# A hybrid encoder layer: the output projection's attention side takes its first two column blocks as a pair, one quarter of it in seven products

## The chip, the cores and the metric

The kernel runs on one core of a Trainium2 chip. A core has a matrix engine (TensorE, PE in the profile, its weight loads are PEld), a vector engine (VectorE, DVE), an activation engine (ScalarE, ACT), a general engine (GpSimd, POOL) and a queue engine that issues DMAs (SyncE, SP). Data lies in SBUF, 128 partitions wide; matmuls write to PSUM, in banks of 128 x 512 float32. The metric is device time in microseconds (us), the median of several runs of one launch.

## The reference

One layer over 256 rows of width 2048. It is a half feed-forward (FFN1), a mixer with two sides that read one projection, an output projection, a second half feed-forward (FFN2) and a gated embedding. The part that matters here is the output projection:

```python
        mixed = jnp.concatenate([rms_norm(y_ssm, out_norm_ssm[i]), rms_norm(y_sb, out_norm_sb[i])], axis=-1)
        x = x + mixed @ w_out[i]
```

`y_ssm` and `y_sb` are 256 x 1024 each (the SSM side and the attention side), `w_out` is 2048 x 2048, all of it in float32. Each side is normalized by its own row-wise root mean square.

## The kernel before

**Products.** A float32 operand is kept as two parts: a high part, and the remainder of the value against it. A product of two operands is three matmuls: high by high, low by high, high by low. Activations lie turned in such pairs (`nhi`, `nlo`, or `hhi`, `hlo`). Weights come in raw quarters, 512 rows by 512 columns as a tile of 128 x 2048 (1 MB), by a DMA on SP (line 331); each quarter has two halves of 128 x 1024. For each half `split` makes the high part by a cast on ACT (line 182) and the remainder by a subtraction on DVE (line 185). The raw tiles are a ring of five, two of which are in use for the rows of x, so that three go round.

**The ring of pairs.** `weight_pair` hands out the tiles for (high, remainder) of a half: four pairs with names `whi`, `wlo` from the pool `wp`, and, where `ring` holds another pool, three more pairs `shi`, `slo` from that one, in turn. The FFNs use all seven; the output projection uses four. `ring` is a list of that other pool and a counter.

**Blocks.** `gemm_block` computes a column block of 512 columns for both row blocks (256 rows) into two PSUM banks of the four single ones (`acc`): for a side of 1024 rows of weights that is two quarters, four halves, and 12 matmuls to a half, 48 in all. `gemm_half` orders them: high weights with both parts of the activations (line 346), then remainder weights with the high part (line 341). `gemm_pair` computes two column blocks at once, in all four single banks.

**Seven products.** The class `Seven` computes two column blocks of one quarter of the rows as a 2 x 2 by 2 x 2 block product in seven products (of 6 matmuls each) instead of eight. It needs sums of the weight tiles (`add`, line 541; one by an accumulating DMA on POOL) and sums of the activations: `whole_rows` (line 470) adds the parts of a quarter, `sum_forms` (line 487) makes four sums of its 128 x 256 pieces and splits them. `Seven.lean` is the variant in single banks: ACT copies (line 606) and DVE adds carry intermediate results out of a bank that is used three times. Its `column` computes a quarter in the ordinary way into the same banks. Line 533 and its neighbours are its matmuls. Before, the mixer's projection for v uses `lean`, in `values()` (its adds stand around line 1638), and FFN1, FFN2 and the last stage use `chunk`, with double banks.

**Order.** The code is recorded, and a scheduler sets the order on each engine. `put_off(n, ...)` puts a piece of work off by n steps of the weight stream; `pin` keeps an instruction where it was written. Each engine then runs its list in order and waits by semaphores.

**Around the change.** `glu` ends the SSM side and gives `yss`, `attn_out` the attention side, `ysb` (each a list of two quarters). `rms(steps, ...)` computes a side's row scale: ones-matmuls, a copy out of PSUM (line 1500) and a chain of small DVE operations (lines 205 to 213). The squares it needs are made on ACT (line 1511) and added on POOL (line 1512). Then `gemm_pair` runs over the SSM side's column blocks 0 and 1, and six `gemm_block` follow: (block 0, attention), (1, attention), (2, SSM), (2, attention), (3, SSM), (3, attention). Behind each of the eight block results x += result * scale runs on DVE (line 1673), which frees the bank. When a column block of x is complete, POOL stores it, and its normalized form for FFN2 is prepared (`n2.block`: transposes on DVE at line 220, splits at lines 195 and 197). FFN2 starts behind the last block.

Of the kernel before, what the change touches and what calls it, by code (L numbers as in the profile page):

```python
# [13 lines left out]
ALU = mybir.AluOpType  # L14
AX = mybir.AxisListType

P = 128
# [9 lines left out]
NB = 512  # L27
# [6 lines left out]
def layer_kernel(ctx: ExitStack, tc: tile.TileContext, a: dict, shapes: dict, out: bass.AP):  # L34
    nc = tc.nc
    _, T, D = shapes["x"]
    F = shapes["ffn1_w_gate"][2]
    SW = shapes["ssm_d"][1]
# [5 lines left out]
    TT = T // P  # L44
# [9 lines left out]
    wp = ctx.enter_context(tc.tile_pool(name="wts", bufs=4))  # L54
# [15 lines left out]
    def com(tag):  # L70
        return get(comp, tag, *{"sg": (1024, 1), "h": (1024, 2), "sq": (NB, 1), "mid": (2048, 1)}[tag])
# [36 lines left out]
    def put_off(steps, fn, *args):  # L108


        def g():
            for _ in range(steps):
                yield
            fn(*args)

        return start(g())
# [183 lines left out]
        return both[:2], both[2:]  # L300

    ring = [None, 0]

    def weight_pair():

        extra, i = ring
        ring[1] += 1
        pool, tags = (extra, ("shi", "slo")) if extra and i % 7 % 2 else (wp, ("whi", "wlo"))
        return [
            pool.tile([P, 2, NB], F32R, tag=s, name=uid(s), bufs=3 if pool is extra else None) for s in tags  # L310
        ]
# [44 lines left out]
    def gemm_block(act, w, n0, nkt, first=()):  # L356

        ps = [acc(), acc()]
        for k0 in range(0, nkt, 4):
            part = act(k0 // 4)  # L360
            quarter = first[k0 // 4] if k0 // 4 < len(first) else weight_halves(w, k0, min(4, nkt - k0), n0)
            for half in list(quarter):
                k = k0 + 2 * half[0]
                gemm_half(ps, (part, half), range(TT), k == 0, k + 2 == nkt, in_turn=first and k0 == 0)
                if first and half[0] == 0 and k0 + 4 < nkt:
                    act(k0 // 4 + 1)
                step()
        return ps

    def gemm_pair(act, ws, nkt):  # L370


        ps = [[acc(), acc()] for _ in ws]
        last = nkt // 4 - 1
        for ks in (range(last - 1), (last - 1,), (last,)):
            for (w, n0), banks in zip(ws, ps):
                for k in ks:
                    part = act(k)
                    for half in list(weight_halves(w, 4 * k, 4, n0)):
# [21 lines left out]
    class Normed:  # L401


        def __init__(self, gain, laid=None, kinds="nnnn", late=1):
            self.early = ND - late
            self.kinds = kinds
            self.gain = gain
            self.laid = laid
            self.parts = {}
            self.mid = None  # L410
            self.ss = [small(ND) for _ in range(TT)]
            self.r = None
# [65 lines left out]
    def sum_forms(pool, u, kind="n"):  # L478

        sums = pool.tile([P, 2, NB], F32, tag="sum", name=uid("rows"), bufs=2)  # L480
        s = sums.rearrange("p j n -> p (j n)").rearrange("p (z j x b) -> p z j x b", z=4, j=2, b=32)
        (a11, a21), (a12, a22) = ([u[:, k : k + 2, 4 * t : 4 * t + 4] for t in range(TT)] for k in (0, 2))
        for z, (x, y, op) in enumerate((
            (a21, a22, ALU.subtract), (s[:, 0], a11, ALU.subtract),
            (a11, a21, ALU.subtract), (a12, s[:, 1], ALU.add),
        )):
            nc.vector.tensor_tensor(out=s[:, z], in0=x, in1=y, op=op)
        both = halves(kind)
        split(*both, sums.rearrange("p j n -> p (j n)").rearrange("p (z t) -> p z t", z=4))
        return both  # L490
# [662 lines left out]
    class Spare:  # L1153
# [5 lines left out]
        def tile(self, shape, dtype, tag, name, bufs):  # L1159
            return get(self.pool, "rt", bufs=3).rearrange("p (j n) -> p j n", n=NB)  # L1160
# [221 lines left out]
    qT, kT, vt = [None, None], [None, None], [None, None]  # L1382
# [223 lines left out]
    q0, k0, v0 = SW, SW + NH * DH, SW + 2 * NH * DH  # L1606
    mix, s5p, atp = ExitStack(), ExitStack(), ExitStack()
    mixp = mix.enter_context(phase("mix"))
    pool = s5p.enter_context(phase("s5"))

    s5_main(pool, mixp)
    forms = {}
# [7 lines left out]
    pool = atp.enter_context(phase("attn"))  # L1620
    zs, ysb = [], []
# [4 lines left out]
    put_off(16, attn_out, pool, 0, ysb, sqa)  # L1626
    vt = [get(pool, f"v{t}") for t in range(TT)]

    def values():
        even, odd = ([v[:, n * NB : (n + 1) * NB] for v in vt] for n in range(2))  # L1630

        def scaled(n):
            for t in range(TT):
                v = vt[t][:, n * NB : (n + 1) * NB]
                pin(nc.scalar.activation(v, v, AF.Copy, scale=nm.rs(t)))

        def halfway(s):
            nc.vector.tensor_tensor(out=even[0], in0=s.bank(2), in1=even[0], op=ALU.add)

        def done(s):  # L1640
            nc.vector.tensor_tensor(out=even[1], in0=s.bank(4), in1=odd[1], op=ALU.add)
            for t in range(TT):
                nc.vector.tensor_tensor(out=odd[t], in0=s.bank(5), in1=odd[t], op=ALU.subtract)
            put_off(1, scaled, 0)

        def ended(s):
            for t, z in enumerate((3, 8)):
                nc.vector.tensor_tensor(out=odd[t], in0=s.bank(z), in1=odd[t], op=ALU.add)
            put_off(1, scaled, 1)

        class Rows:

            def tile(self, shape, dtype, tag, name, bufs):
                return com("h").rearrange("p (j n) -> p j n", n=NB)

        s = Seven(nm, forms.get, ((w_in, v0), (w_in, v0 + NB)), Rows(), None)
        s.column(0, (0, 1, 3))
        s.lean(2, even[0], *odd, halfway, done)
        s.column(1, (0, 1, 3), True)
        put_off(0, ended, s)  # L1660
# [3 lines left out]
    yss, rss = glu(pool, zs)  # L1664
    rsb = rms(9, sqa, NH * DH)
    KS = SW // NB
    sides = [a["w_out"][:, side * KS : (side + 1) * KS] for side in range(2)]
    both = gemm_pair(lambda k: yss[k], [(sides[0], n * NB) for n in range(2)], SW // P)
    for n, side in ((0, 0), (1, 0), (0, 1), (1, 1), (2, 0), (2, 1), (3, 0), (3, 1)):
        y, r = ((yss, rss), (ysb, rsb))[side]  # L1670
        ps = next(both) if n < 2 and not side else gemm_block(lambda k: y[k], sides[side], n * NB, SW // P)
        for t in range(TT):
            nc.vector.scalar_tensor_tensor(
                out=xt[t][n], in0=ps[t], scalar=r[0][:, t : t + 1], in1=xt[t][n], op0=ALU.mult, op1=ALU.add
            )
        if side:
            for t in range(TT):
                nc.gpsimd.dma_start(scr_x[t * P : (t + 1) * P, n * NB : (n + 1) * NB], xt[t][n])
            put_off(0 if n == ND - 1 else 2, n2.block, n)
    atp.close()  # L1680
    mix.close()

# [96 lines left out]
    t = 0  # L1779
# [159 lines left out]
```

## Time and profile before

| | |
|---|---|
| median of 3 runs | 1812.14 us (1811.14 to 1813.1) |
| the profiled execution | 1811.75 us, span 1810.0 us |
| SSM pair's last matmuls end | 956.54 us |
| attention block 0 begins, block 1, (2, SSM), (2, attention), (3, SSM) | 956.61, 968.18, 979.07, 989.95, 1000.83 us |
| FFN2's first matmul | 1022.59 us |
| DVE busy, 956 to 1022 | 50.28 us of 66.00 |
| a weight quarter of `w_out`, from issue to landing | 4.6 to 6.6 us, median 5.0 |

A row of the timeline reads: start, duration, engine, line, operation, output <- inputs with shape and type, how many were put together, and in brackets the idle time before and what ended it. A row of a group reads: line, engine, operation, names, shapes and count, then busy time and mean duration, then the idle time just before these instructions and what ended it. Starts of long neighbouring DVE operations are some 0.08 us closer than their durations, since the end of one overlaps the start of the next.

### The profile page before, as it was taken

How to read it: one execution, taken by the hardware profiler on the slowest of the kernel's cores; microseconds unless marked ns; L12 is line 12 of the kernel's file. 1: busy time of each engine (PE TensorE's matmuls, PEld its weight loads, DVE VectorE, ACT ScalarE, POOL GpSimd, SP SyncE). 2: the span in 40 equal slices, each digit the busy share in tenths (PEclk: the TensorE clock that was granted, in tenths of full speed). 3: DMA queues.
4: the chain of work that ended last, by engine and by line, in shares of the span. 5: the costliest groups of instructions: out<-in, count | busy, mean ns of one | idle time of the engine just before them, and what ended most of it. 6: DMA issues, size and time to landing. Idle time of an engine off the chain costs nothing.

```text
span 1810.0 us, 24253 instructions
## 1 busy us (share of the span) xinstructions
PE 1803.4 (100%) x8902; PEld 1494.9 (83%) x8902; DVE 1598.2 (88%) x1870; ACT 1077.4 (60%) x1253; POOL 132.7 (7%) x194
## 2 busy tenths in 40 slices
PE   9999999999999999999999999999999999999998
PEld 7888888888888888888898888888888888888887
DVE  7998889999998898887867899999999999889775
ACT  7445456556565666466895566555565566567664
POOL 0020100000000001112221000000000000000000
PEclk9999999999999999999999999999999999999999
DMA  9599867787776666765646777786767786666563
GB/s 377 209 310 303 253 226 233 238 270 223 258 267 221 193 238 222 257 240 179 203 155 211 242 284 235 259 263 230 233 232 245 238 272 244 223 207 226 198 244 128
DMA packets 108087, 429.46 MB, mean 237 GB/s; under 512 B 24544, under 2 KB 48384, under 8 KB 65568
## 3 DMA queue, kind: packets, MB, share of 16 engines
q1 hardware_dynamic: 95808, 390.10, 61.1%
q0 software_dynamic: 11872, 37.50, 9.6%
q8 instruction: 70, 1.15, 0.3%
q14 instruction: 49, 0.40, 0.1%
q10 hardware_dynamic: 288, 0.31, 0.1%
HBM read 372.41 MB, written 10.88 MB: 212 GB/s over the span
## 4 chain that ended last, share of the span: by engine, by line
PE 98%; DMA 1%; DVE 0%; SPq 0%; ACT 0%; issue 0%; DVEq 0%; ACTq 0%
PE acc L346 31%; PE acc L341 16%; PE aux L346 15%; PE aux L341 8%; PE acc L530 5%; PE acc L535 5%; PE acc L533 5%; PE aux L533 3%; PE aux L535 3%; PE aux L530 3%; DMA raw<-in_ffn_w_gate 1%; PE aux L1318 0%; PE acc L1575 0%; PE acc L1570 0%; PE acc L1566 0%; PE aux L1263 0%
## 5 line engine op out<-in xcount | busy, mean ns | idle before, releaser
L185 DVE TENSOR_TENSOR wlo<-raw,whi 128x1024 fp32r<-128x1024 f32 x478 | 577.1, 1221 | 103.9 <-ACT whi L182 101.2
L182 ACT CAST whi<-raw 128x1024 fp32r<-128x1024 f32 x478 | 496.4, 1050 | 285.2 <-PE acc L346 166.1
L346 PE MATMUL acc<-whi,nhi 128*128 128x512 f32 x852 | 334.1, 393 | 0.6 <-ACT whi L182 0.5
L346 PE MATMUL acc<-whi,nlo 128*128 128x512 f32 x852 | 331.5, 390 | 0.0
L341 PE MATMUL acc<-wlo,nhi 128*128 128x512 f32 x852 | 240.9, 389 | 0.0
L185 DVE TENSOR_TENSOR slo<-raw,shi 128x1024 fp32r<-128x1024 f32 x186 | 226.4, 1217 | 16.0 <-ACT shi L182 15.7
L182 ACT CAST shi<-raw 128x1024 fp32r<-128x1024 f32 x186 | 195.3, 1050 | 62.2 <-DMA raw<-in_ffn_w_down 23.2
L346 PEld LDWEIGHTS acc<-whi,nhi 128*128 128x128 f32 x852 | 159.9, 188 | 35.7 <-ACT whi L182 0.9
L341 PEld LDWEIGHTS acc<-wlo,nhi 128*128 128x128 f32 x852 | 159.9, 188 | 33.6 <-DVE wlo L185 0.2
L346 PEld LDWEIGHTS acc<-whi,nlo 128*128 128x128 f32 x852 | 160.3, 188 | 32.6
L182 ACT CAST whi<-sum 128x1024 fp32r<-128x1024 f32 x79 | 83.2, 1053 | 156.8 <-DVE sum L541 138.8
L182 ACT CAST shi<-sum 128x1024 fp32r<-128x1024 f32 x59 | 62.2, 1053 | 101.5 <-DVE sum L541 86.8
L634 POOL DMA_DIRECT2D raw<-raw x45 | 39.3, 873 | 1041.6 <-DVE sum L541 691.1
L541 DVE TENSOR_TENSOR sum<-sum,raw 128x1024 f32<-128x1024 f32 x92 | 112.3, 1220 | 0.9
L185 DVE TENSOR_TENSOR wlo<-sum,whi 128x1024 fp32r<-128x1024 f32 x79 | 96.3, 1221 | 5.2 <-ACT whi L182 4.5
L346 PE MATMUL aux<-whi,nhi 128*128 128x512 f32 x244 | 95.0, 390 | 0.0
L346 PE MATMUL aux<-whi,nlo 128*128 128x512 f32 x244 | 95.0, 389 | 0.0
L341 PE MATMUL aux<-wlo,nhi 128*128 128x512 f32 x244 | 75.1, 389 | 0.0
L185 DVE TENSOR_TENSOR slo<-sum,shi 128x1024 fp32r<-128x1024 f32 x59 | 72.1, 1221 | 1.0 <-ACT shi L182 0.5
L346 PE MATMUL acc<-whi,hhi 128*128 128x512 f32 x156 | 60.7, 389 | 0.0
L346 PE MATMUL acc<-whi,hlo 128*128 128x512 f32 x156 | 60.7, 389 | 0.0
L541 DVE TENSOR_TENSOR sum<-raw,raw 128x1024 f32<-128x1024 f32 x46 | 56.1, 1219 | 4.0 <-DMA raw<-in_ffn_w_down 3.1
(423 smaller groups left out, 3531.2 us busy)
## 6 DMA issues: line engine op xcount, KB each, us to landing
raw<-in_ffn_w_up SPq DMA_DIRECT2D x88, 1024.0 KB, 5.5
raw<-in_ffn_w_down SPq DMA_DIRECT2D x88, 1024.0 KB, 4.8
raw<-in_ffn_w_gate SPq DMA_DIRECT2D x86, 1024.0 KB, 7.1
raw<-in_w_in SPq DMA_DIRECT2D x32, 1024.0 KB, 5.6
raw<-raw POOLq DMA_DIRECT2D x48, 512.0 KB, 5.9
raw<-in_w_out SPq DMA_DIRECT2D x16, 1024.0 KB, 5.0
raw<-in_w_ple_gate SPq DMA_DIRECT2D x16, 1024.0 KB, 5.0
hT<-mid SPq DMA_DIRECT2D x160, 64.0 KB, 4.5
```

Of the source, the lines that this page charges most:

```text
L182: copy = nc.scalar.copy(hi, src)
L185: rest = nc.vector.tensor_tensor(out=lo, in0=src, in1=hi.bitcast(F32), op=ALU.subtract)
L341: nc.tensor.matmul(ps[t], lhsT=lh, rhs=lo[:, j, cols], start=False, stop=stop and j == 1)
L346: nc.tensor.matmul(ps[t], lhsT=(ahi, alo)[i][:, 2 * h + j, t * P : (t + 1) * P], rhs=hi[:, j, cols], start=start and j == 0 and i == 0, st ...
L530: nc.tensor.matmul(ps, lhsT=lh[j], rhs=hi[:, j], start=begin and j == 0, stop=False, skip_group_check=joined)
L533: nc.tensor.matmul(ps, lhsT=ll[j], rhs=hi[:, j], start=False, stop=False, skip_group_check=joined)
L535: nc.tensor.matmul(ps, lhsT=lh[j], rhs=lo[:, j], start=False, stop=z in final and j == 1, skip_group_check=joined)
L541: nc.vector.tensor_tensor(out=t, in0=x, in1=y, op=ALU.add)
L634: nc.gpsimd.dma_start(b12, b22, accum_op=ALU.add)
```

## The change

Two things change in the output projection, and the rest moves behind them.

The ring gets six pairs instead of four: `Lent` hands out two more pairs from the tiles of q and k (`q0`, `k0`, `q1`, `k1`), which are no longer used by then, and `extra_of` replaces the fixed seven. Behind the output projection it is set back.

The attention side's blocks 0 and 1 become one pair, `first_two`: the second quarter of the rows by `column` for both blocks (2 x 24 matmuls), the first quarter by `lean` (7 products of 6 matmuls), between the two columns. The forms of `ysb[0]` are made ahead of it, and both `gathered` of the SSM pair are called ahead of it too, with what was the loop's body before. The results are added up in the tiles of v, which are free by then, and x += result * scale follows as before.

```diff
     ring = [None, 0]
+    extra_of = [7, 7]
...
-        pool, tags = (extra, ("shi", "slo")) if extra and i % 7 % 2 else (wp, ("whi", "wlo"))
+        pool, tags = (extra, ("shi", "slo")) if extra and i % extra_of[0] % 2 and i % extra_of[0] < extra_of[1] else (wp, ("whi", "wlo"))
...
-    both = gemm_pair(lambda k: yss[k], [(sides[0], n * NB) for n in range(2)], SW // P)
-    for n, side in ((0, 0), (1, 0), (0, 1), (1, 1), (2, 0), (2, 1), (3, 0), (3, 1)):
-        y, r = ((yss, rss), (ysb, rsb))[side]
-        ps = next(both) if n < 2 and not side else gemm_block(lambda k: y[k], sides[side], n * NB, SW // P)
+    class Lent:
+        def __init__(self):
+            self.tags = ["q0", "k0", "q1", "k1"]
+            self.i = 0
+
+        def tile(self, shape, dtype, tag, name, bufs):
+            self.i += 1
+            return mixp.tile(shape, dtype, tag=self.tags[self.i % 4 - 1], name=name, bufs=1)
+
+    def gathered(n, side, ps):
+        r = (rss, rsb)[side]
         for t in range(TT):
             nc.vector.scalar_tensor_tensor(
                 out=xt[t][n], in0=ps[t], scalar=r[0][:, t : t + 1], in1=xt[t][n], op0=ALU.mult, op1=ALU.add
...
+    def first_two():
+        even, odd = ([v[:, n * NB : (n + 1) * NB] for v in vt] for n in range(2))
+
+        def halfway(s):
+            nc.vector.tensor_tensor(out=even[0], in0=s.bank(2), in1=even[0], op=ALU.add)
+
+        def done(s):
+            nc.vector.tensor_tensor(out=even[1], in0=s.bank(4), in1=odd[1], op=ALU.add)
+            for t in range(TT):
+                nc.vector.tensor_tensor(out=odd[t], in0=s.bank(5), in1=odd[t], op=ALU.subtract)
+            put_off(1, gathered, 0, 1, even)
+
+        def ended(s):
+            for t, z in enumerate((3, 8)):
+                nc.vector.tensor_tensor(out=odd[t], in0=s.bank(z), in1=odd[t], op=ALU.add)
+            gathered(1, 1, odd)
+
+        forms = {}
+        s = Seven(lambda k: ysb[k], forms.get, ((sides[1], 0), (sides[1], NB)), Rows(), None)
+        forms[0] = sum_forms(s.pool, whole_rows(s.pool, ysb[0]), "h")
+        for n in range(2):
+            gathered(n, 0, next(both))
+        s.column(0, (1,))
+        s.lean(0, even[0], *odd, halfway, done)
+        s.column(1, (1,), True)
+        put_off(0, ended, s)
+
+    ring[:], extra_of[:] = [Lent(), 0], [6, 4]
+    both = gemm_pair(lambda k: yss[k], [(sides[0], n * NB) for n in range(2)], SW // P)
+    first_two()
+    for n, side in ((2, 0), (2, 1), (3, 0), (3, 1)):
+        y = (yss, ysb)[side]
+        gathered(n, side, gemm_block(lambda k: y[k], sides[side], n * NB, SW // P))
+    ring[0], extra_of[:] = None, [7, 7]
```

`Rows`, which gives `Seven` a common buffer `h` for its sums, moves out of `values()` so that both can use it.

What becomes of the order is seen on three places. First DVE, from the copy of a mean square out of PSUM to the first x += result * scale of the SSM pair. Before (`wlo` is a weight remainder, `sm` the small operands of the scale, `acc` the bank, `x` the rows):

```order
L1500 COPY sm_8504<-aux_8501 128x2
L185 TENSOR_TENSOR wlo_8585<-raw_8578,whi_8584 128x1024
L205 TENSOR_SCALAR sm_8506<-sm_8504 128x2
L208 RECIPROCAL sm_8508<-sm_8508 128x2
L210 TENSOR_TENSOR sm_8511<-sm_8508 128x2
L211 TENSOR_TENSOR sm_8511<-sm_8511,sm_8506 128x2
L212 TENSOR_SCALAR sm_8511<-sm_8511 128x2
L213 TENSOR_TENSOR sm_8508<-sm_8508,sm_8511 128x2
L1673 SCALAR_TENSOR_TENSOR x_4227<-acc_8372,sm_8508,x_4227 128x512
```

The same place on DVE after the change (`h_8642`, `h_8667`, `h_8691` are the weight sums t1, t2, t4; `slo_8680` is a remainder in a lent tile, the one that `slo_8536` of the SSM pair's last half used before it):

```order
L205 TENSOR_SCALAR sm_8517<-sm_8515 128x2
L185 TENSOR_TENSOR wlo_8657<-h_8642,whi_8656 128x1024
L542 TENSOR_TENSOR h_8667<-h_8642,raw_8640 128x1024
L208 RECIPROCAL sm_8519<-sm_8519 128x2
L542 TENSOR_TENSOR h_8691<-h_8667,raw_8638 128x1024
L210 TENSOR_TENSOR sm_8522<-sm_8519 128x2
L185 TENSOR_TENSOR wlo_8670<-raw_8638,whi_8669 128x1024
L211 TENSOR_TENSOR sm_8522<-sm_8522,sm_8517 128x2
L185 TENSOR_TENSOR slo_8680<-h_8667,shi_8679 128x1024
L212 TENSOR_SCALAR sm_8522<-sm_8522 128x2
L213 TENSOR_TENSOR sm_8519<-sm_8519,sm_8522 128x2
L1684 SCALAR_TENSOR_TENSOR x_4227<-acc_8383,sm_8519,x_4227 128x512
```

One operation of 128 x 1024 stood there, and now five do, two of them the sums t2 and t4.

Second PE, at the seam from the SSM pair to the attention side. Before:

```order
L341 MATMUL acc_8375<-wlo_8525,nhi_8344 128x512
L346 MATMUL acc_8576<-whi_8580,nhi_8122 128x512
L346 MATMUL acc_8576<-whi_8580,nlo_8123 128x512
L346 MATMUL acc_8577<-whi_8580,nhi_8122 128x512
L346 MATMUL acc_8577<-whi_8580,nlo_8123 128x512
```

And after:

```order
L342 MATMUL acc_8386<-slo_8536,nhi_8344 128x512
L347 MATMUL acc_8597<-whi_8589,nhi_8551 128x512
L347 MATMUL acc_8597<-whi_8589,nlo_8552 128x512
L342 MATMUL acc_8597<-wlo_8590,nhi_8551 128x512 x2
L347 MATMUL acc_8604<-whi_8589,nhi_8551 128x512
```

The attention side now begins with its second quarter (`nhi_8551`, where `nhi_8122` was the first), a row block at a time.

Third DVE at the start of FFN2, from the last x += result * scale on (`mid` are turned rows, `nlo` of `rows` the remainder of a sum form, `wlo` of `raw` remainders of FFN2's first weights). Before:

```order
L1673 SCALAR_TENSOR_TENSOR x_4227<-acc_9014,sm_8619,x_4227 128x512
L1673 SCALAR_TENSOR_TENSOR x_4228<-acc_9015,sm_8619,x_4228 128x512
L220 STREAM_TRANSPOSE mid_8992<-x_4227 128x4x4x32
L220 STREAM_TRANSPOSE mid_8992<-x_4228 128x4x4x32
L185 TENSOR_TENSOR wlo_9185<-raw_9178,whi_9184 128x1024
L455 TENSOR_REDUCE sm_9209<-sm_111 128x1
```

And after:

```order
L1684 SCALAR_TENSOR_TENSOR x_4227<-acc_9035,sm_8630,x_4227 128x512
L1684 SCALAR_TENSOR_TENSOR x_4228<-acc_9036,sm_8630,x_4228 128x512
L220 STREAM_TRANSPOSE mid_9009<-x_4227 128x4x4x32
L185 TENSOR_TENSOR nlo_9163<-rows_9157,nhi_9162 128x1024
L220 STREAM_TRANSPOSE mid_9009<-x_4228 128x4x4x32
L185 TENSOR_TENSOR wlo_9216<-raw_9213,whi_9215 128x1024
L185 TENSOR_TENSOR wlo_9220<-raw_9213,whi_9219 128x1024
L456 TENSOR_REDUCE sm_9244<-sm_111 128x1
```

A form's remainder, which stood ahead of the last block's results, now stands between the two transposes, and two weight remainders stand where one did.

More of the change, by code (lines that the diff above doesn't have):

```diff
@@ L1627, in layer_kernel @@
     vt = [get(pool, f"v{t}") for t in range(TT)]
+    class Rows:
+        def tile(self, shape, dtype, tag, name, bufs):
+            return com("h").rearrange("p (j n) -> p j n", n=NB)
     def values():
@@ L1649, in ended @@
             put_off(1, scaled, 1)
-        class Rows:
-            def tile(self, shape, dtype, tag, name, bufs):
-                return com("h").rearrange("p (j n) -> p j n", n=NB)
         s = Seven(nm, forms.get, ((w_in, v0), (w_in, v0 + NB)), Rows(), None)
@@ L1667, in layer_kernel, with tile @@
     sides = [a["w_out"][:, side * KS : (side + 1) * KS] for side in range(2)]
-    both = gemm_pair(lambda k: yss[k], [(sides[0], n * NB) for n in range(2)], SW // P)
-    for n, side in ((0, 0), (1, 0), (0, 1), (1, 1), (2, 0), (2, 1), (3, 0), (3, 1)):
-        y, r = ((yss, rss), (ysb, rsb))[side]
-        ps = next(both) if n < 2 and not side else gemm_block(lambda k: y[k], sides[side], n * NB, SW // P)
+    class Lent:
+        def __init__(self):
+            self.tags = ["q0", "k0", "q1", "k1"]
+            self.i = 0
+        def tile(self, shape, dtype, tag, name, bufs):
+            self.i += 1
+            return mixp.tile(shape, dtype, tag=self.tags[self.i % 4 - 1], name=name, bufs=1)
+    def gathered(n, side, ps):
+        r = (rss, rsb)[side]
         for t in range(TT):
```

## The prediction, made before the changed kernel ran

> **What bounds the kernel now.** I read the page's totals first, then its clock slices and the chain that ended last.
>
> ```profile
> span 1810.0 us, 24253 instructions
> ...
> PE 1803.4 (100%) x8902; PEld 1494.9 (83%) x8902; DVE 1598.2 (88%) x1870; ACT 1077.4 (60%) x1253; POOL 132.7 (7%) x194
> ...
> PEclk9999999999999999999999999999999999999999
> ...
> PE 98%; DMA 1%; DVE 0%; SPq 0%; ACT 0%; issue 0%; DVEq 0%; ACTq 0%
> ```
>
> PE never stops: its busy time is the span, at an undiminished granted clock, and the chain is PE for 98%. So a matmul taken away counts in full, and any new wait of PE counts in full too. DVE is second with 88%. The view of PE's waits says how little PE waits for others:
>
> ```profile
> PE aux L252 <- POOL ones L125: 1.1, 1, 1.1
> PE acc L346 <- ACT whi L182: 0.5, 1, 0.5
> ```
>
> Next the stretch of the change, by windows (columns: length, then busy time of PE, PE's weight loads, DVE, ACT, POOL, the clock, DMA).
>
> ```profile
> 956.00:1022.00 66.00, 65.92 (x293) 54.19 (x292) 50.28 (x66) 33.44 (x47) 3.32 (x6) 1.00 0.68 227
> ```
>
> PE is full; DVE has 66.00 − 50.28 = 15.7 us left over. PE's timeline gives the pace and the two seams:
>
> ```profile
> 955.47 1.07 PE L341 MATMUL acc<-wlo,nhi 128*128 128x512 f32 x4
> 956.61 0.47 PE L346 MATMUL acc<-whi,nhi 128*128 128x512 f32 x1
> ...
> 968.18 0.39 PE L346 MATMUL acc<-whi,nhi 128*128 128x512 f32 x1
> ...
> 979.07 0.39 PE L346 MATMUL acc<-whi,nhi 128*128 128x512 f32 x1
> ```
>
> The SSM pair ends at 955.47 + 1.07 = 956.54, and the attention side's column block 0 follows at 956.61. A block of 48 matmuls lasts 979.07 − 968.18 = 10.89 us, so one costs 0.2269 us.
>
> **What it removes.** Column blocks 0 and 1 of the attention side had 2 × 48 = 96 matmuls. Now: two columns of 24 and seven products of 6, 90 in all. Six fewer: 6 × 0.2269 = **−1.36 us**. Block 0 before took 968.18 − 956.61 = 11.57 us, of which four small matmuls of the next mean square are some 0.36; the other 0.3 us are little hiccups at its beginning. They go if operands are waiting when PE comes late: **−0.3 us**.
>
> **What it adds.** Durations come from the same operations elsewhere: the pair for v (862 to 877), and FFN2's forms.
>
> ```profile
> L185 DVE TENSOR_TENSOR wlo<-raw,whi 128x1024 fp32r<-128x1024 f32 x25 | 30.3, 1218 | 11.3 <-ACT whi L182 11.3
> L470 DVE TENSOR_TENSOR whole<-hhi,hlo 128x1024 f32<-128x1024 f32 x1 | 1.2, 1225 | 0.0
> L487 DVE TENSOR_TENSOR rows<-whole 128x256 f32<-128x256 f32 x2 | 0.8, 416 | 0.0
> ...
> 862.05 1.23 DVE L541 TENSOR_TENSOR h<-raw,raw 128x1024 f32<-128x1024 f32 x1 [0.49 <-DMA raw<-in_w_in]
> ...
> 876.39 0.68 DVE L1638 TENSOR_TENSOR v<-acc,v 128x512 f32<-128x512 f32 x1
> ...
> L606 ACT COPY v<-acc 128x512 f32<-128x512 f32 x1 | 0.6, 587 | 0.0
> ...
> L599 POOL DMA_DIRECT2D raw<-raw x1 | 0.9, 940 | 3.5 <-ACT sp L1449 3.5
> ```
>
> DVE: a whole (1.22), four form subtractions (4 × 0.42), the form's remainder (1.22), t1, t2, t4 (3.7), three more weight remainders (eleven instead of eight, 3.7) and six adds (6 × 0.68): about 15.6 us. ACT: one form cast and three weight casts of 1.05, three copies of 0.59: 6.0 us. POOL: one issue of 0.94, landing while PE waits or works on other products; I count nothing for it, and 0.9 us if a product stood waiting for it. About 5.3 us of DVE's share (whole, forms, t1) falls before 956, the other 10.3 into a stretch with 15.7 to spare. As a sum DVE holds. What costs is **where** it stands.
>
> **The new wait.** PE's first attention matmul writes a bank that the first `gathered` of the SSM pair must read. DVE before, up to that operation:
>
> ```profile
> 940.85 6.79 DVE L185 TENSOR_TENSOR wlo<-raw,whi 128x1024 fp32r<-128x1024 f32 x5 [1.69 <-ACT whi L182]
> 949.54 1.66 DVE L197 SCALAR_TENSOR_TENSOR nlo<-aux,gains,nhi 128x256 fp32r<-128x256 f32 x4 [1.90 <-ACT nhi L195]
> 951.12 0.16 DVE L1500 COPY sm<-aux 128x2 f32<-128x2 f32 x1
> 951.19 1.22 DVE L185 TENSOR_TENSOR wlo<-raw,whi 128x1024 fp32r<-128x1024 f32 x1
> ...
> 954.05 0.17 DVE L208 RECIPROCAL sm<-sm 128x2 f32<-128x2 f32 x1 [1.02 <-ACT sm L207]
> ...
> 955.71 2.73 DVE L1673 SCALAR_TENSOR_TENSOR x<-acc,sm,x 128x512 f32<-128x512 f32 x4
> ```
>
> Before, one large operation stands between the mean square's copy and `gathered`; after, five (the order shown with the change), each 1.14 us from start to start (951.19 to 952.33 in the DVE timeline). They are not free to go early. t1 needs the attention pair's second quarter, whose raw buffer is refilled only when `slo_8536`, a remainder of the SSM side, has been taken. The last of the five, `slo_8680`, goes into the lent slot that PE reads until the end of the SSM pair. The rows for the walk:
>
> ```profile
> 938.54 1.33 ACT L1511 ACTIVATE sqp<-h 128x256 f32<-128x256 f32 x4
> ...
> 939.09 4.06 POOL L1512 TENSOR_TENSOR sqg<-sqg,sqp 128x256 f32<-128x256 f32 x4 [12.99 <-ACT sqp L1511]
> 951.76 3.70 POOL L1512 TENSOR_TENSOR sqa<-sqa,sqp 128x256 f32<-128x256 f32 x4 [8.60 <-ACT sqp L1511]
> ...
> DMA to landing us min/median/max: 4.6/5.0/6.6
> ```
>
> 1. One more weight cast stands ahead of the squares on ACT, so they end at 938.54 + 1.33 + 0.95 = 940.8; the form's buffer is theirs until then.
> 2. DVE then does four form subtractions (1.5) and three remainders at the 6.79 / 5 = 1.36 that this row shows beside POOL's adds (4.1): `slo_8536` is done at about 946.4.
> 3. The quarter lands 5.0 later, 951.4; t1 takes until 952.5; four nlo (1.66), the copy and a small one: 954.3.
> 4. Five large operations, 5 × 1.14 = 5.7, small ones between them 0.4, and 1.0 for POOL's second group of adds, now beside them: 961.4.
> 5. `gathered` needs 0.70 (2.73 / 4): PE resumes at 962.1 and not at 956.61: **+5.5 us**.
>
> Lower end: were everything early, `slo_8680` still follows PE's end at 956.54: 1.22, two small ones and 0.70 give 959.1, so 2.5 us. Upper end: 1.6 more for a DMA at its longest (6.6) and 1.0 for another cast in the way: 8.1. I take the walk's 5.5, each step of which has a row. What lies behind the waiting DVE operation is all of PE's work; nothing else covers it.
>
> A rule bears on step 4. The Trainium skill, "SBUF — State Buffer", section "SBUF: two separate sides", says that DVE operations with two SBUF inputs and GpSimd exclude each other for whole instructions. The row agrees in kind (1.36 instead of 1.14 beside the adds); taken in full, all 3.70 us of adds would block DVE, and the sum would be 2.7 us higher than with my 1.0.
>
> **Behind it.** The middle of the pair: product 3 gets a bank that the `halfway` add frees, queued on DVE behind the late remainders: **+0.4 us** (0 if PE's delay has let DVE catch up). FFN2's start: two transposes are split by a form remainder that before had been done, and remainders of its first weights stand behind it.
>
> ```profile
> 1022.56 1.41 DVE L1673 SCALAR_TENSOR_TENSOR x<-acc,sm,x 128x512 f32<-128x512 f32 x2 [0.56 <-PE acc L341]
> ...
> 1037.55 1.22 DVE L185 TENSOR_TENSOR slo<-sum,shi 128x1024 fp32r<-128x1024 f32 x1
> ...
> 1038.82 0.73 PE L535 MATMUL acc<-slo,hhi 128*128 128x512 f32 x2
> ```
>
> DVE does 1.2 to 2.4 us more between the last `gathered` and that remainder. Already before, the remainder that ends at 1037.55 + 1.22 = 1038.77 is what the matmul at 1038.82 takes. Some idle slivers of DVE and late starts of PE cover part: **+0.6 us**, from 0 to 2.
>
> **Sum**, against the profiled execution's 1811.75 (its span and 1.75 around it; 0.39 under the median 1812.14): 1811.75 − 1.36 − 0.3 + 5.5 + 0.4 + 0.6 = **1816.6 us**.
>
> **Rivals.**
> - *The slot alone decides* (the other side: not slower by 0.2%). If the second quarter lands early enough for DVE to have the first four behind it, from about 948.5 on, only the lower end is left: 1811.75 − 1.66 + 2.5 = 1812.6, up to 1815 where it comes halfway. For: step 3 rests on one landing time and step 2 on an order in which each 1.36 may be 1.14. Against: ACT's one cast more is certain in the order.
> - *PE restarts slowly.* The kernel's first matmuls:
>
> ```profile
> 1.14 3.78 PE L252 MATMUL aux<-ones 128*128 128x128 f32 x16 [1.14 <-POOL ones L125]
> 4.80 1.19 PE L346 MATMUL acc<-whi,nhi 128*128 128x512 f32 x2
> 5.79 0.98 PE L346 MATMUL acc<-whi,nlo 128*128 128x512 f32 x2
> 6.61 0.63 PE L341 MATMUL acc<-wlo,nhi 128*128 128x512 f32 x2
> ```
>
>   Four large ones need 6.61 − 4.80 = 1.81 us where 4 × 0.2269 = 0.91 is the pace, though the clock column reads 1.00 there. A pause of 5.5 us may bring that back: 0.9 us at least, and 2.7 if half pace lasts the 5.47 us from 1.14 to 6.61; the middle gives 1816.6 + 1.8 = 1818.4. Against: no pause of that length lies inside the kernel before, so nothing shows that one suffices. The Trainium skill, "TensorE: Matmul & The Clock Gate", Part 1, speaks for it: an idle window of about 3.4 us halves the clock until a busy window has passed; an estimate from that page is 1.7 us.
> - *DVE becomes the bound up to FFN2.* If its 15.7 us are mostly waits that cannot be filled, FFN2's first weights are late by 3 more: 1819.6. Against: the pair's delay itself gives DVE 3.8 us.
> - *Only the products count.* If the walk is wrong by its whole 5.5 and PE finds its bank free: 1811.75 − 1.66 = 1810.1. Against: the slot's lower end.
>
> **Chances.** Forecast 0.45, slow restart 0.20, slot alone 0.22, DVE the bound 0.08, products only 0.05. Within 0.2% of the median (about what a measurement of this kernel can tell from no change) means 1808.5 to 1815.8: slot alone, products only but for 0.02, and 0.07 of the forecast's lower tail: 0.32. Faster 0.02, slower 0.66. The range runs from the lower end (1812.6) to 1811.75 − 1.66 + 8.1 + 0.4 + 2 = 1820.6, that is 1812.5 to 1820.6; it leaves out the products alone and the rivals' far ends.
>
> **What would show it.** Right: in the changed trace PE idles once, between the SSM pair's last remainder product and the first attention matmul, 4 to 7 us, released by DVE's first `gathered`, and ahead of that on DVE five 128x1024 operations without gaps. From there to FFN2's first matmul PE needs 90 + 192 matmuls at 0.2269 = 64.0 us and little more. The slow restart shows in the first four matmuls behind the pause, at 0.4 us and more. Wrong: a wait of 2.5 or less there, a wait of PE at the raw quarters or for the accumulating DMA, or a loss of over 2 us behind FFN2's start.

## The result, and the profile after

The changed kernel takes **1822.84 us** (median of 6 runs, 1821.65 to 1824.35) against 1811.76 us for the kernel before in the same comparison: ratio 1.0062, 95% interval 1.0051 to 1.0072. The sign was forecast; the size was not: 6.2 us above the forecast and 2.2 above the range. The profiled execution took 1824.35 us, the slowest of the six, 12.6 above the one before (1811.75).

The page of the changed kernel, with the lines that answer to those of before:

```profile
span 1822.6 us, 24262 instructions
...
PE 1804.4 (99%) x8896; PEld 1495.1 (82%) x8896; DVE 1612.3 (88%) x1888; ACT 1080.2 (59%) x1260; POOL 136.3 (7%) x195
...
PE 89%; DMA 3%; DVE 3%; ACT 2%; SPq 2%; issue 1%; ACTq 0%; DVEq 0%
```

PE has its six matmuls fewer (8896 for 8902), and the chain that ended last now leaves PE for 11% of the span. PE's waits from 900 to 1100:

```profile
PE acc L347 <- DVE x L1684: 7.7, 1, 7.7
PE aux L342 <- DVE wlo L185: 1.1, 1, 1.1
PE acc L536 <- DVE slo L185: 0.9, 1, 0.9
PE acc L531 <- ACT shi L182: 0.5, 1, 0.5
```

One wait at the seam, released by `gathered` (now line 1684), and three at FFN2's start. PE's timeline at the seam, and below it the window behind the pause (length, busy times of PE, weight loads, DVE, ACT, POOL, then the granted clock):

```profile
955.69 1.07 PE L342 MATMUL acc<-slo,nhi 128*128 128x512 f32 x4
964.43 0.76 PE L347 MATMUL acc<-whi,nhi 128*128 128x512 f32 x1 [7.67 <-DVE x L1684]
...
965.42 0.63 PE L347 MATMUL acc<-whi,nhi 128*128 128x512 f32 x1
...
967.95 0.40 PE L347 MATMUL acc<-whi,nhi 128*128 128x512 f32 x1
```

```profile
964.00:968.00 4.00, 3.57 (x9) 2.86 (x10) 2.25 (x4) 0.00 (x0) 0.00 (x0) 0.51 0.28 115
```

PE resumes at 964.43, not at 956.61, and its first eight matmuls take 967.95 − 964.43 = 3.52 us, where 8 × 0.2269 = 1.82 is the pace: 1.70 lost, at a granted clock of 0.51. DVE ahead of that, and POOL beside it:

```profile
941.05 1.31 DVE L488 TENSOR_TENSOR h<-h 128x256 f32<-128x256 f32 x2 [0.74 <-ACT sqp L1512]
942.29 0.96 DVE L488 TENSOR_TENSOR h<-h,h 128x256 f32<-128x256 f32 x1
943.17 1.76 DVE L185 TENSOR_TENSOR wlo<-raw,whi 128x1024 fp32r<-128x1024 f32 x1
944.85 0.41 DVE L488 TENSOR_TENSOR h<-h,h 128x256 f32<-128x256 f32 x1
...
946.32 1.21 DVE L185 TENSOR_TENSOR slo<-raw,shi 128x1024 fp32r<-128x1024 f32 x1
...
952.36 1.23 DVE L542 TENSOR_TENSOR h<-raw,raw 128x1024 f32<-128x1024 f32 x1 [0.19 <-DMA raw<-in_w_out]
...
955.20 1.22 DVE L185 TENSOR_TENSOR wlo<-h,whi 128x1024 fp32r<-128x1024 f32 x1
956.33 1.22 DVE L542 TENSOR_TENSOR h<-h,raw 128x1024 f32<-128x1024 f32 x1
...
957.59 1.63 DVE L542 TENSOR_TENSOR h<-h,raw 128x1024 f32<-128x1024 f32 x1
959.14 0.68 DVE L210 TENSOR_TENSOR sm<-sm 128x2 f32<-128x2 f32 x1
959.75 1.21 DVE L185 TENSOR_TENSOR wlo<-raw,whi 128x1024 fp32r<-128x1024 f32 x1
...
961.48 1.21 DVE L185 TENSOR_TENSOR slo<-h,shi 128x1024 fp32r<-128x1024 f32 x1
...
963.53 2.73 DVE L1684 SCALAR_TENSOR_TENSOR x<-acc,sm,x 128x512 f32<-128x512 f32 x4
```

```profile
955.79 7.49 POOL L1513 TENSOR_TENSOR sqa<-sqa,sqp 128x256 f32<-128x256 f32 x4 [0.46 <-ACT sqp L1512]
```

The five large operations stand there as the order said, from 955.20 on. Three of the small ones take 0.68 us where 0.16 is usual, and one sum 1.63 where 1.22 is usual, beside POOL's four adds, which take 7.49 us here and took 3.70 before. The lent slot held nothing up: PE was done with it at 955.69 + 1.07 = 956.76, and `slo` starts at 961.48.

At FFN2's start the chain runs over SP, ACT, DVE and PE (one line of each, and one of DVE ahead of the remainder):

```profile
1026.86 0.53 SPq L332 DMA_DIRECT2D raw<-in_ffn_w_up  x1
...
1033.40 1.06 ACT L182 CAST whi<-raw 128x1024 fp32r<-128x1024 f32 x1 [5.16 <-DMA raw<-in_ffn_w_up]
...
1035.43 1.23 DVE L185 TENSOR_TENSOR nlo<-rows,nhi 128x1024 fp32r<-128x1024 f32 x1 [1.02 <-ACT nhi L182]
...
1037.20 2.32 DVE L185 TENSOR_TENSOR wlo<-raw,whi 128x1024 fp32r<-128x1024 f32 x2
...
1038.44 0.73 PE L342 MATMUL aux<-wlo,hhi 128*128 128x512 f32 x2 [1.11 <-DVE wlo L185]
```

FFN2's first `w_up` quarter is issued 4.0 us ahead of FFN2's first matmul (1030.83); before it was 8.5 (1014.12 against 1022.59):

```profile
1014.12 0.53 SPq L331 DMA_DIRECT2D raw<-in_ffn_w_up  x1
```

DVE's order has a part in it too: the cast is done at 1033.40 + 1.06 = 1034.46, and the remainder starts at 1037.20, behind a form's remainder, for whose cast DVE idles 1.02 us, and a transpose, which the order puts ahead of it.

**Where the 12.6 us lie.** Matching matmuls of the two traces gives the delay at each: 7.8 at the seam, 8.2 at FFN2's first matmul (1.7 for the slow matmuls, less 1.4 for the six and 0.3 for the hiccups; 0.4 are small gaps in the pair, none of them in the list of waits), about 11.3 from 1060 on, 11.7 at 1225, 12.6 at the end. The last 0.9 come in the final stage, far from the change.

### The profile page after: what moved, and what is told of

It reads as the page before. It is cut to its first block, busy times and chain, and to the rows that moved or that the text cites. A ratio compares the mean times of both kernels' runs of the same rounds, so it can differ in the third digit from the quotient of the medians.

```text
span 1822.6 us, 24262 instructions
## 1 busy us (share of the span) xinstructions
PE 1804.4 (99%) x8896; PEld 1495.1 (82%) x8896; DVE 1612.3 (88%) x1888; ACT 1080.2 (59%) x1260; POOL 136.3 (7%) x195
## 4 chain that ended last, share of the span: by engine, by line
PE 89%; DMA 3%; DVE 3%; ACT 2%; SPq 2%; issue 1%; ACTq 0%; DVEq 0%
PE acc L347 28%; PE aux L347 14%; PE acc L342 14%; PE aux L342 7%; PE acc L531 5%; PE acc L536 5%; PE acc L534 5%; PE aux L536 3%; PE aux L534 3%; PE aux L531 3%; SPq L233 1%; DMA raw<-in_w_out 1%; DMA raw<-in_ffn_w_gate 1%; ACT whi L182 1%; DMA h<-mid 1%
## 5 line engine op out<-in xcount | busy, mean ns | idle before, releaser
L185 DVE TENSOR_TENSOR wlo<-raw,whi 128x1024 fp32r<-128x1024 f32 x467 | 564.3, 1223 | 100.2 <-ACT whi L182 96.6
L182 ACT CAST whi<-raw 128x1024 fp32r<-128x1024 f32 x467 | 484.7, 1050 | 278.3 <-PE acc L347 140.9
L347 PE MATMUL acc<-whi,nhi 128*128 128x512 f32 x796 | 312.8, 394 | 9.5 <-DVE x L1684 7.7
L347 PE MATMUL acc<-whi,nlo 128*128 128x512 f32 x796 | 310.2, 390 | 0.0
L185 DVE TENSOR_TENSOR slo<-raw,shi 128x1024 fp32r<-128x1024 f32 x197 | 240.4, 1220 | 20.3 <-ACT shi L182 19.4
L182 ACT CAST shi<-raw 128x1024 fp32r<-128x1024 f32 x197 | 206.7, 1049 | 72.1 <-DMA raw<-in_ffn_w_down 20.2
L342 PE MATMUL acc<-wlo,nhi 128*128 128x512 f32 x796 | 226.9, 390 | 0.1
L342 PEld LDWEIGHTS acc<-wlo,nhi 128*128 128x128 f32 x796 | 149.6, 188 | 31.6 <-DVE wlo L185 0.5
L185 DVE TENSOR_TENSOR wlo<-sum,whi 128x1024 fp32r<-128x1024 f32 x79 | 96.6, 1225 | 5.2 <-ACT whi L182 4.5
L347 PE MATMUL acc<-shi,nlo 128*128 128x512 f32 x164 | 63.9, 389 | 0.0
L347 PE MATMUL acc<-shi,nhi 128*128 128x512 f32 x164 | 63.8, 389 | 0.0
```

What stands on the lines that cost most here:

```text
L182: copy = nc.scalar.copy(hi, src)
L185: rest = nc.vector.tensor_tensor(out=lo, in0=src, in1=hi.bitcast(F32), op=ALU.subtract)
L342: nc.tensor.matmul(ps[t], lhsT=lh, rhs=lo[:, j, cols], start=False, stop=stop and j == 1)
L347: nc.tensor.matmul(ps[t], lhsT=(ahi, alo)[i][:, 2 * h + j, t * P : (t + 1) * P], rhs=hi[:, j, cols], start=start and j == 0 and i == 0, st ...
```

## The experiments

Each was compared with the kernel before on the same chip; its medians in these comparisons lie between 1811.25 and 1811.86. "Offset" is the delay of the same matmul against the trace of before. Ahead of the change, at 950, it lies between −1.0 and 0.2 us from trace to trace, so what a stretch costs is the difference of two offsets.

### A pause alone, in the kernel before

One or four extra operations of 128x1024 on DVE ahead of `gathered`; they write v's dead tiles.

```diff
+            if n == 0 and not side:
+                for _ in range(4):
+                    more = nc.vector.scalar_tensor_tensor(
+                        out=vt[0], in0=vt[0], scalar=r[0][:, 0:1], in1=vt[1], op0=ALU.mult, op1=ALU.add
+                    )
+            if n < 2 and not side:
+                held.enter_context(tc.issue_after(more.ins))
```

With one:

> The kernel before, with one operation of 128x1024 on VectorE ahead of gathered (it writes the dead tiles of v). Theory (each such operation moves PE's first attention product by its length, and a short pause costs only itself): a pause of about 1.2 us, matmuls behind it at 0.23 us from start to start, 1812.5 to 1813.5. Rival (any pause slows the matmuls behind it): 1814 or more.

With four, twice: the profiled execution of the first took 7,609 us and is used for nothing, so the trace is that of the second, a single run:

> The kernel before, with four such operations, and two weight remainders between them. Theory (a pause of several us is followed by some 3.5 us of matmuls at 0.43 us each): a pause of 6 to 7 us and 1.6 us for the slow matmuls, 1818.5 to 1821 if the delay is not made up later. Rival (the slow matmuls in the changed kernel come from something else, as the ports): no slow matmuls, 1817.5 to 1818.5.

> The kernel before with four operations ahead of gathered, once more, for a trace without a disturbance. Theory (a long pause slows the matmuls behind it): a pause of 6 to 7 us, then 3 to 3.5 us of matmuls at 0.43 us from start to start, and 1819 to 1823. Rival (no slowing): all matmuls at 0.23 us, the time above the kernel before that of the pause alone.

One: 1812.48 us (1.0003, 0.9993 to 1.0012), not to be told from no change. Four: 1821.97 us (1.0049, 1.0031 to 1.0067), and 1820.54 in the single run; the pause and the slow stretch behind it are both longer than expected. PE's timeline with one, then with four:

```profile
957.66 0.47 PE L346 MATMUL acc<-whi,nhi 128*128 128x512 f32 x1 [1.28 <-DVE x L1681]
957.97 0.39 PE L346 MATMUL acc<-whi,nlo 128*128 128x512 f32 x1
```

```profile
963.32 0.77 PE L346 MATMUL acc<-whi,nhi 128*128 128x512 f32 x1 [7.26 <-DVE x L1681]
...
968.37 0.40 PE L346 MATMUL acc<-whi,nhi 128*128 128x512 f32 x1
```

The pause of 1.28 leaves the pace alone. That of 7.26 is followed by twelve matmuls in 968.37 − 963.32 = 5.05 us instead of 2.72: 2.3 lost. The offset in the single run's trace is 8.8 from there to the end, so nothing is made up and nothing more is lost. A pause plus a slow restart accounts for 9 us without any pair.

### GpSimd's adds left out

The four adds of squares of the attention side's second quarter are not done.

```diff
-            nc.gpsimd.tensor_tensor(out=total, in0=total, in1=sq, op=ALU.add)
+            if not skip:
+                nc.gpsimd.tensor_tensor(out=total, in0=total, in1=sq, op=ALU.add)
```

> The changed kernel without GpSimd's four adds of squares of the attention side's second quarter (they are left out, so the attention side's mean square lacks that quarter). Theory (beside these adds VectorE's three small operations take 0.68 us in place of 0.16 and one sum 1.63 in place of 1.22): the pause shrinks by about 2 us, to 5.5 to 6, and the time by as much: 1820 to 1821.5. Rival (the adds only fill time in which VectorE waits for something else): pause 7.5, 1822.8.

1821.14 us, as expected, and PE's wait:

```profile
PE acc L347 <- DVE x L1685: 5.9, 1, 5.9
```

5.9 in place of 7.7: the adds' share of the pause is 1.8 us. From the first of the five large operations to `gathered` DVE takes 961.53 − 955.00 = 6.53 us, in place of 963.53 − 955.20 = 8.33.

### The ring alone, and the pair alone

Six pairs with plain blocks in the old order:

```diff
-    first_two()
-    for n, side in ((2, 0), (2, 1), (3, 0), (3, 1)):
+    for n, side in ((0, 0), (1, 0), (0, 1), (1, 1), (2, 0), (2, 1), (3, 0), (3, 1)):
         y = (yss, ysb)[side]
-        gathered(n, side, gemm_block(lambda k: y[k], sides[side], n * NB, SW // P))
+        gathered(n, side, next(both) if n < 2 and not side else gemm_block(...))
```

> Six weight pairs in the ring, but the attention side as plain blocks in the old order. Theory (the sums of the seven products cost the time, the ring does not): no pause at the seam, 1811 to 1813. Rival (the lent tiles make PE wait, or more weights taken early crowd VectorE or ScalarE): a pause of over 2 us, 1814 or more.

1813.86 us (1.0012, 1.0003 to 1.0021): between the two expectations. PE waits 1.6 us at the seam: an early weight cast that waits for its transfer stands on ACT ahead of the split of the attention side's second quarter.

The pair with four pairs in the ring:

```diff
-    ring[:], extra_of[:] = [Lent(), 0], [6, 4]
```

> The pair with seven products, with the old ring of four pairs. Theory (what stands ahead of gathered decides, and here six large operations stand there, one of them behind a slot that PE holds until the SSM pair ends): a pause of 6 to 8 us, 1820 to 1824. Rival (the lent slot of the last of the five decides): the pause shrinks to 3 us or less, 1813 to 1816.

1823.28 us (1.0066, 1.0051 to 1.0081). The pause is 5.4 us, 2.3 shorter than in the changed kernel and shorter than expected:

```profile
962.19 0.77 PE L347 MATMUL acc<-whi,nhi 128*128 128x512 f32 x1 [5.42 <-DVE x L1684]
...
967.43 0.39 PE L347 MATMUL acc<-whi,nhi 128*128 128x512 f32 x1
```

Behind it twelve matmuls take 967.43 − 962.19 = 5.24 us instead of 2.72, so 2.5 are lost, and FFN2's start loses 3.1 as in the changed kernel. The medians of the two do not differ beyond their spread. Of the two candidates, what stands ahead of `gathered` makes the pause, with or without lent slots.

### Gathered first

DVE's operations of `lean` are ordered behind the four `gathered` operations of the SSM pair.

```diff
-        s.lean(0, even[0], *odd, halfway, done)
+        with tc.issue_after(gathered.last.ins):
+            s.lean(0, even[0], *odd, halfway, done)
```

> The changed kernel, with VectorE's operations of the seven products ordered behind the four gathered operations of the SSM pair. Theory (the pause is VectorE's queue ahead of gathered): PE's pause at the seam falls from 7.7 us to under 1, with it the slow matmuls behind it (1.6 us), while the loss of about 2.5 us at FFN2's start stays: 1813 to 1815. Rival (VectorE is simply too full for the added work, the order only moves the wait): the pause comes back inside the pair or behind it, 1820 to 1823.

1822.6 us, where the rival had it, though the seam did as the theory said in the main. PE's waits from 940 to 1100:

```profile
PE acc L347 <- DVE x L1684: 2.4, 1, 2.4
PE acc L531 <- ACT shi L182: 1.8, 1, 1.8
PE acc L347 <- ACT whi L182: 1.5, 1, 1.5
PE aux L342 <- DVE wlo L185: 0.7, 1, 0.7
PE acc L531 <- ACT v L607: 0.6, 1, 0.6
PE acc L342 <- DVE wlo L185: 0.5, 1, 0.5
PE acc L531 <- ACT whi L182: 0.4, 1, 0.4
PE acc L347 <- ACT shi L182: 0.3, 1, 0.3
PE acc L531 <- DVE v L1696: 0.2, 1, 0.2
```

The seam is mended (2.4 for 7.7, full pace behind it), and the offset at the end of the projection is 2.7 us. Then 8.8 us are lost in FFN2's first 30. Its `w_up` quarter is issued at 1026.84, within 0.02 us of the changed kernel's, although PE is 5.5 us ahead of it at the end of the projection. PE's waits there (1.8, 1.5, 0.7, 0.5 and 0.4) are all for casts and remainders of weights, and slow matmuls follow the last of them.

### Transfers on GpSimd's queue

The transfers of turned rows (line 233), on which FFN2's inputs depend, are issued by SP among the weight loads. Each edit gives those of some x blocks to GpSimd:

```diff
-                turn_quarters(out, mid, 4 if soon else 6)
+                turn_quarters(out, mid, 4 if soon else 6, nc.gpsimd if n < 3 and self.gain == "ffn2_norm" else nc.sync)
```

With blocks 0 and 1, in the changed kernel and with gathered first:

> The changed kernel, with the 32 transfers of turned rows of x blocks 0 and 1 issued by GpSimd in place of SyncE, so that no weight quarter stands behind them. Theory (FFN2's first weights come late because their loads are queued behind those transfers): the 2.5 us that PE loses at FFN2's start go, the pause of 7.7 us at the seam stays: 1819 to 1821. Rival (VectorE's order at FFN2's start costs them): 1822 to 1824.

> Both edits: VectorE's operations of the seven products behind gathered, and the 32 transfers on GpSimd's queue. Theory (what gathered first saved at the seam was lost again to weights that came late, since SyncE's queue holds them to a fixed time): the seam's pause stays at 2.4 us and FFN2's start loses under 1 us: 1812.5 to 1815. Rival (VectorE is full, or the loads are late for another reason, as raw tiles that the pair holds): 1818 or more.

1828.18 and 1824.86 us: both theories miss, and so does the first rival; the second's range holds. `w_up` still stands behind block 2's transfers, and GpSimd's come later, with DVE's splits of blocks 0 and 1 waiting for them ahead of other work. With blocks 0 to 2, and with block 2 alone, gathered first in both:

> Gathered first, and all 48 transfers of turned rows of x blocks 0, 1 and 2 on GpSimd's queue. In the run with 32 of them there, the second of FFN2's weight quarters still stood behind block 2's transfers on SyncE (issued 1021.3, landed 1029.6), and block 2 itself came late. Theory (what counts is that FFN2's first quarters stand behind transfers in SyncE's queue): with none there, w_up is issued by 1016, FFN2's start loses under 1.5 us, and 1813.5 to 1816 is left. Rival (the splits of the late blocks 0 and 1 on VectorE hold up the gathered of block 2 and with it everything behind, whatever the queue): FFN2's start still loses 3 us or more, 1818 to 1825.

> Gathered first, and only block 2's 16 transfers on GpSimd's queue; blocks 0 and 1 stay on SyncE. Theory: FFN2's quarters no longer stand behind block 2's transfers, but the last two quarters of w_out still stand behind those of blocks 0 and 1, so w_gate is issued at 1016 and w_up at 1021: FFN2's start loses 2 to 4 us, 1816 to 1819. Rival (block 2's late gathered alone makes the weights late): as with gathered first alone, 1822.

1818.45 us (1.0038, 1.0024 to 1.0052) and 1820.59 us. With three blocks `w_up` is issued at 1014.8 and the offset at FFN2's first matmul is 1.2 us; then PE waits 3.1 us for a weight sum (DVE and ACT) and restarts slowly, 5.0 us lost in all. That is the rival's time and loss: early weights alone do not mend FFN2's start. The second number lies between theory and rival. Against gathered first alone (1822.6, no run under 1821.15) less is lost with all three blocks' transfers off SP's queue (no run above 1818.96); with block 2's alone the runs overlap. The same queue in the changed kernel as it is, and in the kernel before:

> The changed kernel as it is, with the 48 transfers on GpSimd's queue and nothing else. Theory (the seam and FFN2's start add up): the pause of 7.7 us and the slow matmuls stay, FFN2's start loses 1 us or less in place of 2.5 to 3: 1820 to 1821.5. Rival (the late transfers of GpSimd's queue, as in the run with 32 of them, cost more than the queue gives): 1824 to 1829.

> The kernel before, with the 48 transfers of x blocks 0 to 2 on GpSimd's queue. Theory (in the kernel before SyncE's queue has room, so the queue is worth nothing there): 1811 to 1812.5. Rivals: the weights were held up there too, under 1810.5; or transfers on GpSimd's queue come so much later that they cost by themselves, over 1813.

1821.11 us, as expected, and 1818.55 us (1.0036, 1.0023 to 1.0049), the second rival: GpSimd's queue costs the kernel before 7.3 us (1811.25 in this comparison). From issue to landing such a transfer takes 4.2 us at the median between 965 and 1022, where it took 3.5 on SP's queue. In the changed kernel PE then has one wait between 900 and 1100:

```profile
PE acc L347 <- DVE x L1684: 7.8, 1, 7.8
```

The offset grows from 7.8 at FFN2's first matmul to 8.5 at 1060 and 8.6 at the end, where with SP's queue it grew from 8.2 to 11.3 and 12.6.

Last, ScalarE's casts of `lean` behind the squares as well, with 48 and with all 64 transfers on GpSimd's queue:

```diff
-        with tc.issue_after(gathered.last.ins):
+        with tc.issue_after(gathered.last.ins), tc.issue_after(add_square.last.ins):
             s.lean(0, even[0], *odd, halfway, done)
```

> As the run before the last, and the casts of the seven products on ScalarE behind the squares of the attention side's second quarter. With gathered first, ScalarE had one cast, which waited for its transfer, ahead of the split of that quarter, and PE still paused 2.4 us. Theory (that cast makes the remaining pause): the pause falls under 1 us, and the time is 1.5 to 2 us under that of gathered first with all transfers on GpSimd's queue. Rival (the chain of the mean square alone makes it): 2.4 us stay.

> Gathered first, ScalarE's casts behind the squares, and all 64 transfers on GpSimd's queue. With 48 there 1.7 us of PE waiting was left at FFN2's start, behind sums of weights. Theory (the last block's 16 transfers on SyncE still stand among FFN2's quarters): that wait shrinks under 1 us, 1812 to 1815. Rival (the sums wait for the accumulating transfer, which is GpSimd's too and now stands behind 16 more): 1816 to 1820.

1816.24 us (1.0029, 1.0019 to 1.0039; nine runs from 1814.13 to 1819.66) and 1817.05 us (1.0029, 1.0018 to 1.0040). The pause falls to 0.9 us, as the theory had it. The offset in the first one's trace goes from −1.0 at 950 to 0.0 at FFN2's first matmul, so what is left of the waits still costs 1.0 us more than the six matmuls save. Then PE waits 1.7 us for a weight sum, and with 64 transfers 3.5, the rival's side. With GpSimd's queue for 48 transfers in both, the median lies under that of the kernel before (1818.55), but the runs overlap and the gain is not shown; with SP's queue nothing tried beats the kernel before.

### Late transfers alone, in the kernel before

```diff
-            put_off(0 if n == ND - 1 else 2, n2.block, n)
+            put_off((6, 3, 2, 0)[n], n2.block, n)
```

> The kernel before, with the preparation of x blocks 0 and 1 for FFN2 put off by four steps and by one step more, so that their 32 transfers come later and closer together, as in the changed kernel, with none of the pair's work. Theory (late and bunched transfers alone make FFN2's first weights late): a loss of 1 to 3 us at FFN2's start, 1812.5 to 1815. Rival (it takes the pair's own work on VectorE and ScalarE): no loss, 1811 to 1812.4.

1813.03 us (1.0009, 0.9999 to 1.0018): in the theory's range, but at the edge of what can be told from nothing. PE's waits at FFN2's start are 0.9 and 0.5 us, where the kernel before has none, and the offset grows by 1.7 us there, so late transfers do cost; but they came less late than in the changed kernel (`w_up` is issued at 1015.24).

## Why the prediction fell short

**What it had right.** The place and the mechanism: one long pause between the SSM pair and the attention side, released by `gathered`, with five large DVE operations ahead of it. Ordering them behind `gathered` takes 5.3 of the 7.7 us away. The lent slot, a rival, held nothing up. The six matmuls are gone from PE's count, and the −0.3 for hiccups and +0.4 for the middle of the pair come to the +0.1 that is left in the trace. That is in part luck: the list shows no wait in the pair, only small gaps are there, and the wait for `halfway` that the +0.4 stood for did not come.

**What put the time outside the range.** The range's upper end held the wait (8.1 against 7.8) but nothing for a slow restart, which cost 1.7, and at most 2 for FFN2's start, which cost 3.1. Three terms failed, as follows.

**The wait, 5.5 against 7.8 us.** The term was mis-sized in the walk's steps 2 and 4, each time by what short DVE operations cost beside POOL's adds. In step 2 the four form subtractions were priced at 1.5, as they run alone; here they took 2.4 (three from 941.05 to 943.17, beside POOL's first adds, and the fourth, behind these, 0.33), and `slo_8536` was done at 947.5, not 946.4. The landing took 4.8, near the 5.0 forecast, and step 4 began 0.9 us late. In step 4 the large operations and the small ones between them were put at 6.1 without the adds and at 1.0 for the adds; the run without the adds shows 6.5, and 1.8 for the adds. The price of 1.0 was one that long operations pay, five times 0.22; but three of the small ones took 0.68 each beside the adds and some 0.15 without. The kernel before had shown it: its five small operations took 955.71 − 954.05 = 1.66 us beside the same adds, one of them so:

```profile
954.88 0.60 DVE L212 TENSOR_SCALAR sm<-sm 128x2 f32<-128x2 f32 x1
```

So 0.9 up to step 4, 0.8 for the adds, 0.4 for the small ones and 0.2 more in step 5 make the 2.3. The rule of the Trainium skill's "SBUF — State Buffer" that the prediction weighed, taken in full, gave 3.7 for the adds, 2.7 above its 1.0; the measured 1.8 lies between. POOL's adds were slowed as well (7.49 us, 3.70 before).

**The restart, 0 against 1.7 us.** The forecast left it to a rival with a chance of 0.20, priced at 1.8. The step that failed is the choice: a pause that was itself forecast at 5.5 us should have carried it. That a pause of this length suffices is shown by the pair with four pairs in the ring: 5.42 us, and 2.5 lost behind it. Pauses of 1.28 us (one extra operation), 1.55 (the ring alone) and 2.40 (gathered first) at the same place left the pace alone, and the 7.26 us in the kernel before show that it needs no pair. The rule that the prediction cited from the Trainium skill's "TensorE: Matmul & The Clock Gate", Part 1, was right at this seam; its estimate of 1.7 us stands beside the measured 1.7, 2.3 and 2.5.

**FFN2's start, 0.6 against about 3.1 us.** The prediction had named a loss of over 2 us there as a sign of being wrong, and it came. It saw DVE's order there and not SP's. In the changed kernel blocks 0 and 1 of x are complete only at the pair's end, close together; their 32 transfers stand on SP ahead of the last `w_out` quarters, which are issued at 1007.89 and 1013.85; the results of block 2, its transfers and the `w_up` quarter behind them follow late. With 48 transfers off SP's queue the offset grows there by 0.7 us in place of 3.1, in one trace each, and the medians differ by 1.7 us (1.2 if each is set against the kernel before in its own comparison). This points to SP's queue for the larger part in the changed kernel, but does not isolate it: with 32 transfers moved the time rose, and with gathered first 5.0 us stayed although `w_up` was issued early. How the loss divides between the late quarters, the late transfers and DVE's order is not settled: each edit moved the others, and late transfers alone cost 1.8 us by the medians, with an interval from nothing to 3.3.

**The rest.** About 0.9 us of the profiled execution's delay arose in the last stage and 0.4 between; six runs put the median 1.5 us below that execution. Its cause stays open.

So: forecast 1816.6, plus 2.3 for the wait, 1.7 for the restart, 2.5 for FFN2's start and 1.3 for that rest, gives 1824.4, against 1824.35 for the execution from which these terms were read. Which of them is smaller in the median, 1822.84, is not known.

## What to carry to other kernels

Where a bank is freed by an engine that also prepares the next stage, look at what the schedule puts between the last result and the operation that frees the bank: work for the new stage that is called later in the code may stand first. Price short operations as they run beside another engine's work, not as they run alone. A pause is not the price of its own length only; behind one of 5.4 us or more PE ran at half pace here. And mending one wait shows the next: with 5.3 us of pause taken away the total did not move, and the trace shows the following stage's `w_up` quarter issued at the same time as without the mending.

## What was not expected of the hardware

After a pause of only 1.81 us, behind three of 0.4 to 0.7 in the 13 us before it, PE ran slow as well (PE's timeline of gathered first, at FFN2's start; 0.43 us from start to start up to 1049.17):

```profile
1044.51 0.50 PE L531 MATMUL acc<-shi,nhi 128*128 128x512 f32 x1 [1.81 <-ACT shi L182]
...
1045.78 0.61 PE L531 MATMUL aux<-whi,nhi 128*128 128x512 f32 x1
1046.18 1.05 PE L536 MATMUL acc<-slo,nhi 128*128 128x512 f32 x2
1047.04 0.63 PE L534 MATMUL aux<-whi,nlo 128*128 128x512 f32 x1
```

The slow matmuls began 1.3 us after the restart (at 1045.78), not at once, and the granted clock from 1046 to 1049 was 0.50. Ahead of it PE had been busy for 2.24 of the 4.50 us from 1040 to 1044.5, so no pause of several us was needed. And GpSimd's queue, which looked free, cost 7.3 us in the kernel before for 48 transfers of 32 KB.
